# A plain step in the up projection, reserved buffers for the down projection, and x2 added earlier

## The chip, the cores and the metric

The kernel runs on one core of a Trainium2 chip. Its engines are TensorE (PE, with its weight loads shown apart as PEld), VectorE (DVE), ScalarE (ACT), GpSimd (POOL) and SyncE (SP, which here issues the DMAs). The metric is the device time of one execution in microseconds. Three runs of the kernel before took 2077.02, 2077.21 and 2078.11 us; the median is 2077.21.

## The reference

One decoder layer on 512 tokens of width 2048, all in float32. Two attentions (sliding window with sinks, and stick-breaking) share one input projection and one output projection, and behind them stands an MLP with squared ReLU:

```python
x = x + jnp.einsum('bse,ed->bsd', mix, w_out[l])
h = rmsnorm(x, norm_mlp_g[l])
u = jnp.einsum('bsd,df->bsf', h, w_up[l])
x = x + jnp.einsum('bsf,fd->bsd', jnp.square(jax.nn.relu(u)), w_down[l])
```

`w_up` is 2048 x 8192, `w_down` 8192 x 2048. The change lies in these two products. Below, x2 is the x that enters the MLP.

## The kernel before

Every float32 factor is split in two float32r parts, hi (a cast on ACT) and lo (the difference, on DVE; `split`, lines 88 to 90), and a product is made of three matmuls: hi x hi, hi x lo, lo x hi.

**Up projection** (lines 784 to 880). Both factors are cut in 2 x 2 blocks, and seven block products replace eight (the Strassen-Winograd scheme). There are G = 32 groups of 256 columns of `w_up`, and in each KP = 8 steps k, one for a pair of 128-row blocks. A step (`u_step`, line 833) does this: every second step issues the weight DMA for four pairs ahead (`u_load`, `st`) and POOL's four sums of weight blocks for two pairs ahead (`u_sums`, `s_`, two buffers); each step splits the weights of step i + 2 (`u_split`: three raw blocks, 128x384, and four sums, 128x512, four buffers of hi and lo in `whl`), then makes 21 matmuls of 256 columns (`u_products`). The other factor lies ready: `h2[k]` with seven blocks in hi and lo, made from x2 by `turn_x2` (line 731) by way of the buffer `hq`. It is scaled by a first estimate `rp` of the norm; the exact factor q2 is applied at the very end.

The four PSUM banks of group g - 1 are finished during the steps of group g: `u_finish` (line 798) is a generator that yields after each piece. It adds the banks up (`e`, `u`), applies ReLU and square on ACT, forms the sums for the next scheme (`a`), splits them (`ah` on ACT, `al` on DVE, 128x1792), and stores them in DRAM (`ac`).

**Down projection** (lines 885 to 1035). Again seven products, P1 to P7, over 2 x 2 blocks. There are NC = 8 chunks c of the 8192 rows, and two halves j of the columns; cj counts both. Each product is 24 matmuls of 512 columns (lines 1015 to 1025). `d_load` brings raw weight blocks (two DMAs of 1 MB for each r), `d_act` one block of activations (1 MB), `d_sum` makes T1 to T4 on POOL, `d_split` the hi and lo parts, one product ahead. `d_take` (line 930) adds a finished bank to the sums in SBUF, one product later. In the last chunk it also adds U2 to three of the four results, and `onto` (line 944) makes result x q2 + x2 on DVE. In that chunk the products P2, P3 and P4 are scaled by q2 as they are added, and the rows are stored.

**What sets the order.** The program is written for a scheduler that keeps dependencies, inserts the waits, and may reorder instructions on an engine; each engine then works strictly in its order. SBUF is handed out by pools, on two stacks, left and right. A pool that takes the place of closed pools waits for their last use. The pools of the down projection (`rw` for raw weights, `t3`, `ab` for activations) lie on the right, where `h2_0` to `h2_5` and the sums of the up projection were:

```python
    finishing = u_finish(G - 1, ps, ew)
    mlp.close()
    ...
    rw = ctx.enter_context(tc.tile_pool(name="rw", bufs=6, side="right", reuse_waits="tile"))
```

The first loads, T1 and the first split are written behind the whole up projection (lines 982 to 989), and the last group's `u_finish` behind the first product of the down projection (line 1027).

Of the kernel before, what the change touches and what calls it, by code (L numbers as in the profile page):

```python
# [20 lines left out]
P = 128  # L21
# [37 lines left out]
def hymba_layer(ctx: ExitStack, tc: tile.TileContext, x, norm_attn_g, w_in, q_norm_g, k_norm_g,  # L59
# [17 lines left out]
           0: even.enter_context(tc.tile_pool(name="big0", bufs=KD // 2))}  # L77
    once = attn.enter_context(tc.tile_pool(name="once", bufs=1, side="right"))
# [282 lines left out]
    oscr = dram.tile([2 * 8, P, T], F32, name="oscr")  # L361
    S = [once.tile([P, T], F32, name=f"S{b}") for b in range(2)]
# [347 lines left out]
    def evac_b(n, t, ps):  # L710
# [4 lines left out]
        junk = xw.tile([P, 512], F32, tag="junk", bufs=2, name=f"j2{n}{t}")  # L715
        nc.scalar.activation(out=junk, in_=xt, func=AF.Square, accum_out=ss2[:, t, n:n + 1])
        xts[n, t] = xt
# [8 lines left out]
        for tt in range(NT) if n == 0 else (t,):  # L726
            xs = xw.tile([P, 512], F32, tag="xs", bufs=8, name=f"xs2_{n}{tt}")
            nc.scalar.mul(out=xs, in_=xts[n, tt], mul=rp[:, tt:tt + 1])
            xts[n, tt] = xs

    def turn_x2(n, kk, banks):

        k = 2 * n + kk
        hq = xw.tile([P, 8, HP], F32, tag="hq", bufs=2, name=f"hq{k}")
        for r in range(2):
# [5 lines left out]
            nc.scalar.mul(out=hq[:, 0::7] if r == 0 else hq[:, 1:3],  # L741
                          in_=tr.rearrange("p (b t) -> p b t", b=2), mul=g)
        for o, a, b in ((3, 7, 0), (4, 2, 3), (5, 2, 7), (6, 1, 4)):
            nc.vector.tensor_tensor(out=hq[:, o], in0=hq[:, a], in1=hq[:, b], op=ALU.subtract)
        hi = hp[k].tile([P, 7, HP], F32R, name=f"h2h{k}")
        lo = hp[k].tile([P, 7, HP], F32R, name=f"h2l{k}")
        split(hq[:, 0:7], hi, lo)
# [36 lines left out]
    def u_products(i, ps):
# [3 lines left out]
        for a, b, n, half in U_PRODUCTS:  # L788
# [9 lines left out]
    def u_finish(g, ps, ew):  # L798
# [13 lines left out]
        nc.vector.tensor_tensor(out=e[:, 3], in0=u[:, 1], in1=y[:, 0], op=ALU.add)  # L812
        a = ew.tile([P, 8, HP], F32, tag="a", name=f"a{g}")
# [40 lines left out]
    odd.close()  # L854
    left = ExitStack()
# [12 lines left out]
    ms2 = sm.tile([P, NT], F32, tag="ms", name="ms_2")  # L868
    nc.vector.tensor_reduce(out=q2, in_=ss2, axis=AX.X, op=ALU.add)
    nc.vector.tensor_scalar(out=ms2, in0=q2, scalar1=1.0 / D, scalar2=EPS, op0=ALU.mult, op1=ALU.add)  # L870
    for _ in range(2):
        nc.vector.tensor_tensor(out=ms2, in0=ms2, in1=rp, op=ALU.mult)
    nc.vector.reciprocal(out=q2, in_=ms2)
    tail.close()
    ew = left.enter_context(tc.tile_pool(name="ew", bufs=1))
    for g in range(1, G):
        finishing = u_finish(g - 1, ps, ew)
        ps = u_banks(g)
        for i in range(g * KP, (g + 1) * KP):
            u_step(i, ps, finishing)  # L880
    finishing = u_finish(G - 1, ps, ew)
    mlp.close()
# [47 lines left out]
    def d_take(q, banks):  # L930
# [32 lines left out]
        if not last:  # L963
            return
# [15 lines left out]
    for cj in range(2 * NC):  # L980
        c, j = divmod(cj, 2)
        if cj == 0:
# [5 lines left out]
            for i in ORDER[1:]:  # L988
                d_act(0, i)
# [69 lines left out]
```

## Time and profile before

| What | Value |
|---|---|
| median of three runs | 2077.21 us |
| the profiled execution | 2076.19 us, of which the span is 2074.5 us |
| PE busy | 2019.0 us (97% of the span), 11652 matmuls |
| DVE busy | 1678.5 us (81%) |
| ACT, POOL busy | 1008.1 us (49%), 1045.7 us (50%) |
| up projection, groups 1 to 31 | about 774 to 1422.6 us |
| down projection | 1427.5 us to the end |

PE is busy nearly throughout, and matmuls overlap (each shows 283 ns where the next starts far earlier), so the busy share of PE says little: what counts is the distance of one matmul's start to the next. An idle time in brackets, or behind a bar, is that of the engine just ahead of the instruction, with what ended it. In the views by stretch the engines come in the order PE, PEld, DVE, ACT, POOL, and behind them the granted clock (1.00 is 2.4 GHz, 0.50 is 1.2), the DMA share and GB/s. The timeline gives starts in microseconds from the span's start. `lo_u` and `hi_u` are the split weights of the up projection, `s_u` POOL's sums, `st_u` raw weights; `lo_d`, `hi_d`, `T` and `st_d` are the same in the down projection, `ad` its activations, `C` and `U` its results, `x2r` a block of x2.

### The profile page before, as it was taken

How to read it: one execution, taken by the hardware profiler on the slowest of the kernel's cores; microseconds unless marked ns; L12 is line 12 of the kernel's file. 1: busy time of each engine (PE TensorE's matmuls, PEld its weight loads, DVE VectorE, ACT ScalarE, POOL GpSimd, SP SyncE). 2: the span in 40 equal slices, each digit the busy share in tenths (PEclk: the TensorE clock that was granted, in tenths of full speed). 3: DMA queues.
4: the chain of work that ended last, by engine and by line, in shares of the span. 5: the costliest groups of instructions: out<-in, count | busy, mean ns of one | idle time of the engine just before them, and what ended most of it. 6: DMA issues, size and time to landing. Idle time of an engine off the chain costs nothing. (4 is left out here: it accounts for less than half of the span.)

```text
span 2074.5 us, 30963 instructions
## 1 busy us (share of the span) xinstructions
PE 2019.0 (97%) x11652; PEld 1722.1 (83%) x11652; DVE 1678.5 (81%) x2038; ACT 1008.1 (49%) x1692; POOL 1045.7 (50%) x904
## 2 busy tenths in 40 slices
PE   8999999999999999999999999998999999999998
PEld 7777777777677889999999999997788888888876
DVE  4468646565775579999999999998889888988999
ACT  6267534544553565555555555554543333333332
POOL 0013322222220137777778787877755555555663
PEclk9999999999999999999999999999999999999999
DMA  6742332223345535656555555658756456456453
GB/s 217 116 133 82 102 96 73 72 92 117 103 140 175 180 109 163 195 186 194 187 188 194 185 196 184 198 183 326 265 208 230 158 206 244 144 204 260 152 187 108
DMA packets 213913, 350.28 MB, mean 169 GB/s; under 512 B 9779, under 2 KB 154372, under 8 KB 206596
## 3 DMA queue, kind: packets, MB, share of 16 engines
q1 hardware_dynamic: 211216, 345.02, 49.1%
q10 hardware_dynamic: 2548, 3.30, 1.4%
q8 instruction: 91, 1.49, 0.3%
q14 instruction: 58, 0.48, 0.1%
HBM read 270.16 MB, written 78.12 MB: 168 GB/s over the span
## 5 line engine op out<-in xcount | busy, mean ns | idle before, releaser
L794 PE MATMUL ps_u<-h2h,lo_u 128*128 128x256 f32 x1792 | 506.7, 283 | 15.7 <-DVE lo_u L90 15.7
L793 PE MATMUL ps_u<-h2l,hi_u 128*128 128x256 f32 x1792 | 506.4, 283 | 2.7 <-DVE h2l L90 2.7
L792 PE MATMUL ps_u<-h2h,hi_u 128*128 128x256 f32 x1792 | 506.3, 283 | 0.6 <-ACT h2h L89 0.6
L769 POOL TENSOR_TENSOR s_u<-st_u 128x256 f32<-128x256 f32 x256 | 254.6, 1015 | 242.3 <-DVE lo_u L90 171.7
L1024 PE MATMUL ps_d<-lo_d,ad 128*128 128x512 f32 x896 | 357.1, 399 | 6.4 <-DVE lo_d L90 6.4
L1023 PE MATMUL ps_d<-hi_d,ad 128*128 128x512 f32 x896 | 356.5, 398 | 6.5 <-DMA ad<-ac 4.9
L794 PEld LDWEIGHTS ps_u<-h2h,lo_u 128*128 128x128 f32 x1792 | 340.1, 190 | 21.9 <-DVE lo_u L90 21.8
L1025 PE MATMUL ps_d<-hi_d,ad 128*128 128x512 f32 x896 | 356.5, 398 | 0.0
L793 PEld LDWEIGHTS ps_u<-h2l,hi_u 128*128 128x128 f32 x1792 | 337.0, 188 | 3.2 <-DVE h2l L90 3.1
L792 PEld LDWEIGHTS ps_u<-h2h,hi_u 128*128 128x128 f32 x1792 | 336.6, 188 | 1.0 <-ACT h2h L89 1.0
L90 DVE TENSOR_TENSOR lo_d<-T,hi_d 128x1024 fp32r<-128x1024 f32 x128 | 244.8, 1924 | 49.4 <-ACT hi_d L89 49.4
L89 ACT CAST hi_u<-s_u 128x512 fp32r<-128x512 f32 x256 | 158.3, 618 | 226.4 <-POOL s_u L769 226.4
L918 POOL TENSOR_TENSOR T<-st_d,T 128x1024 f32<-128x1024 f32 x64 | 162.6, 2543 | 208.9 <-DVE lo_d L90 207.7
L90 DVE TENSOR_TENSOR lo_u<-s_u,hi_u 128x512 fp32r<-128x512 f32 x256 | 248.0, 969 | 8.6 <-ACT hi_u L89 8.4
L89 ACT CAST hi_d<-T 128x1024 fp32r<-128x1024 f32 x128 | 134.3, 1051 | 214.0 <-PE ps_d L1025 196.8
L1024 PEld LDWEIGHTS ps_d<-lo_d,ad 128*128 128x128 f32 x896 | 169.4, 189 | 49.9 <-DVE lo_d L90 8.9
L1023 PEld LDWEIGHTS ps_d<-hi_d,ad 128*128 128x128 f32 x896 | 169.6, 189 | 48.8 <-ACT a L816 4.9
L90 DVE TENSOR_TENSOR lo_u<-st_u,hi_u 128x384 fp32r<-128x384 f32 x256 | 202.3, 790 | 4.6 <-ACT hi_u L89 4.6
L1025 PEld LDWEIGHTS ps_d<-hi_d,ad 128*128 128x128 f32 x896 | 169.6, 189 | 41.1
L90 DVE TENSOR_TENSOR lo_d<-st_d,hi_d 128x1024 fp32r<-128x1024 f32 x96 | 190.1, 1996 | 13.3 <-ACT hi_d L89 13.2
L89 ACT CAST hi_d<-st_d 128x1024 fp32r<-128x1024 f32 x96 | 100.9, 1051 | 163.5 <-PE ps_d L1025 163.5
L769 POOL TENSOR_TENSOR s_u<-s_u,st_u 128x256 f32<-128x256 f32 x128 | 140.5, 1098 | 0.0
(220 smaller groups left out, 3823.6 us busy)
## 6 DMA issues: line engine op xcount, KB each, us to landing
st_u<-in_w_up SPq DMA_DIRECT2D x128, 512.0 KB, 4.4
st_d<-in_w_down SPq DMA_DIRECT2D x64, 1024.0 KB, 6.1
ad<-ac SPq DMA_DIRECT2D x56, 1024.0 KB, 6.4
ac<-ah SPq DMA_DIRECT2D x32, 896.0 KB
ac<-al SPq DMA_DIRECT2D x32, 896.0 KB, 4.8
st_qk<-in_w_in SPq DMA_DIRECT2D x64, 256.0 KB, 3.0
st_o<-in_w_out SPq DMA_DIRECT2D x32, 512.0 KB, 4.2
st_qa<-in_w_in SPq DMA_DIRECT2D x16, 512.0 KB, 3.8
```

Source lines behind the costliest of these rows:

```text
L89: nc.scalar.copy(out=hi, in_=st)
L90: nc.vector.tensor_tensor(out=lo, in0=st, in1=hi.bitcast(F32), op=ALU.subtract)
L769: nc.gpsimd.tensor_tensor(out=o, in0=a, in1=b, op=op)
L792: nc.tensor.matmul(o, wh[:, a], hh[:, b], start=first, stop=False, skip_group_check=True)
L793: nc.tensor.matmul(o, wh[:, a], hl[:, b], start=False, stop=False, skip_group_check=True)
L794: nc.tensor.matmul(o, wl[:, a], hh[:, b], start=False, stop=(k == KP - 1), skip_group_check=True)
L918: nc.gpsimd.tensor_tensor(out=o, in0=raw[cj, a, h], in1=raw[cj, b, h], op=ALU.subtract)
L1023: nc.tensor.matmul(o, al, bh[:, kk], start=first, stop=False, skip_group_check=True)
L1024: nc.tensor.matmul(o, al, bl[:, kk], start=False, stop=False, skip_group_check=True)
L1025: nc.tensor.matmul(o, ar, bh[:, kk], start=False, stop=end, skip_group_check=True)
```

## The change

- The step k = PLAIN = 7 of each up group uses eight plain block products in place of seven. `h2[7]` has four blocks, its weights are split as they are (one split of 128x512), POOL makes sums for k = 6 alone in that pair, and `u_finish` gets one more addition.
- Two weight buffers (`rwa`) and one activation buffer (`aba`) are set aside on the left from the start of the up projection; the right keeps four and six (`rwb`, `abb`). `hq` has one buffer instead of two, and the squares are written where `xs` goes later.
- The first weight loads, the first activation block, T1 and the first split are written into the steps 1, 4 and 6 of the last up group.
- x2, multiplied by t2 = 1/q2, is added to the sums after P2 of chunk 2, P3 of chunk 3, P4 of chunk 4 and P7 of chunk 5 (DVE); in the last chunk ACT scales the results by q2 in place.
- In the very last product the matmuls of the first bank come ahead of those of the second.
- Small tiles named pad shift what lies behind them.

```diff
+    edge = ctx.enter_context(tc.tile_pool(name="edge", bufs=1, side="right"))
+    edge.tile([P, 120], F32, name="pad_right")
...
+    const.tile([P, 32], F32, name="pad_left")
+    sm.tile([P, 32], F32, tag="pad", bufs=1, name="pad_small")
...
+    PLAIN = KP - 1
...
-        junk = xw.tile([P, 512], F32, tag="junk", bufs=2, name=f"j2{n}{t}")
-        nc.scalar.activation(out=junk, in_=xt, func=AF.Square, accum_out=ss2[:, t, n:n + 1])
+        xs = xw.tile([P, 512], F32, tag="xs", bufs=8, name=f"xs2_{n}{t}")
+        nc.scalar.activation(out=xs, in_=xt, func=AF.Square, accum_out=ss2[:, t, n:n + 1])
...
-        hq = xw.tile([P, 8, HP], F32, tag="hq", bufs=2, name=f"hq{k}")
+        hq = xw.tile([P, 8, HP], F32, tag="hq", bufs=1, name=f"hq{k}")
...
+        nb = 4 if k == PLAIN else 7
+        hi = hp[k].tile([P, nb, HP], F32R, name=f"h2h{k}")
+        lo = hp[k].tile([P, nb, HP], F32R, name=f"h2l{k}")
+        if k != PLAIN:
+            for o, a, b in ((3, 7, 0), (4, 2, 3), (5, 2, 7), (6, 1, 4)):
+                nc.vector.tensor_tensor(out=hq[:, o], in0=hq[:, a], in1=hq[:, b], op=ALU.subtract)
+        split(hq[:, 0:nb], hi, lo)
...
             s_ = sp.tile([P, 2, 4, P], F32, tag="s", name=f"s_u{i}")
+            if i % (KP // 2) == PLAIN // 2:
+                w, s_ = w[:, 0:1], s_[:, 0:1]
...
+            if i % KP == PLAIN:
+                split(w, hi[:, 0:4], lo[:, 0:4])
+                return
...
+    U_PLAIN = ((1, 0, 1, 0), (3, 1, 1, 0), (1, 3, 3, 0), (3, 2, 3, 0), (0, 0, 3, 1), (2, 1, 3, 1), (0, 3, 0, 1),
+               (2, 2, 0, 1))
...
-        for a, b, n, half in U_PRODUCTS:
+        for a, b, n, half in U_PLAIN if k == PLAIN else U_PRODUCTS:
...
         nc.vector.tensor_tensor(out=e[:, 3], in0=u[:, 1], in1=y[:, 0], op=ALU.add)
+        nc.vector.tensor_tensor(out=e[:, 3], in0=e[:, 3], in1=w[:, 1], op=ALU.add)
...
     odd.close()
+    rwa = ctx.enter_context(tc.tile_pool(name="rwa", bufs=2))
+    aba = ctx.enter_context(tc.tile_pool(name="aba", bufs=1))
     left = ExitStack()
...
-                st = rw.tile([P, 2, 1024], F32, tag="rw", name=f"st_d{cj}{r}{h}")
+                pool = rwa if (4 * cj + 2 * r + h) % 6 < 2 else rwb
+                st = pool.tile([P, 2, 1024], F32, tag="rw", name=f"st_d{cj}{r}{h}")
...
-            a = ab.tile([P, 2, 4, HP], F32R, tag="a", name=f"ad{c}{i}")
+            a = (aba if i == ORDER[0] else abb).tile([P, 2, 4, HP], F32R, tag="a", name=f"ad{c}{i}")
...
-            nc.vector.scalar_tensor_tensor(out=o, in0=o, scalar=q2[:, t:t + 1], in1=xt, op0=ALU.mult, op1=ALU.add)
+            nc.vector.scalar_tensor_tensor(out=o, in0=xt, scalar=t2[:, t:t + 1], in1=o, op0=ALU.mult, op1=ALU.add)
...
+            if (c, name) in ((2, "P2"), (3, "P3"), (4, "P4"), (5, "P7")):
+                onto(o, n, t)
         if not last:
             return
         for tt in range(2):
             if name == "P1":
-                n, t = column(0, tt, 0)
-                onto(sums_d["C11", j, tt], n, t)
+                o = sums_d["C11", j, tt]
+                nc.scalar.mul(out=o, in_=o, mul=q2[:, tt:tt + 1])
...
                     nc.gpsimd.tensor_tensor(out=o, in0=o, in1=sums_d["U2", j, tt], op=ALU.add)
-                    onto(o, n, t)
+                    nc.scalar.mul(out=o, in_=o, mul=q2[:, t:t + 1])
...
+    for g in range(1, G):
+        finishing = u_finish(g - 1, ps, ew)
+        ps = u_banks(g)
+        for k in range(KP):
+            if g == G - 1:
+                if k == 1:
+                    d_load(0, 0)
+                    d_act(0, ORDER[0])
+                elif k == 4:
+                    d_sum(0, "T1")
+                elif k == 6:
+                    d_split(0)
+            u_step(g * KP + k, ps, finishing)
+    finishing = u_finish(G - 1, ps, ew)
+    mlp.close()
+    rwb = ctx.enter_context(tc.tile_pool(name="rwb", bufs=4, side="right", reuse_waits="tile"))
+    t3 = ctx.enter_context(tc.tile_pool(name="t3", bufs=2, side="right", reuse_waits="tile"))
+    abb = ctx.enter_context(tc.tile_pool(name="abb", bufs=6, side="right", reuse_waits="tile"))
...
         if cj == 0:
-            d_load(0, 0)
-            d_act(0, ORDER[0])
-            d_sum(0, "T1")
-            d_split(0)
+            d_act(0, ORDER[1])
             d_load(0, 1)
-            for i in ORDER[1:]:
+            for i in ORDER[2:]:
                 d_act(0, i)
...
+            at_end = q == 14 * NC - 1
+            for h, tt in sorted(((h, tt) for h in range(2) for tt in range(2)), key=lambda x: x[::-1] if at_end else x):
+                bh, bl = parts_d[q, h]
```

## Rows read from the trace of the kernel before

**Rows 1.** The page's part 1: engine, busy us (share of the span), instructions.

```profile
PE 2019.0 (97%) x11652; PEld 1722.1 (83%) x11652; DVE 1678.5 (81%) x2038; ACT 1008.1 (49%) x1692; POOL 1045.7 (50%) x904
```

**Rows 2.** Busy time by stretch: window, length, engines' busy us, clock, DMA.

```profile
814.00:1422.60 608.60, 592.86 (x4892) 586.85 (x4891) 584.39 (x730) 337.58 (x579) 465.84 (x461) 1.00 0.59 190
1422.60:1485.00 62.40, 52.99 (x211) 41.50 (x210) 54.10 (x32) 30.24 (x35) 47.48 (x16) 0.95 0.91 357
1485.00:2018.00 533.00, 533.00 (x2276) 428.50 (x2276) 474.62 (x373) 203.24 (x198) 305.59 (x113) 1.00 0.54 200
2018.00:2074.50 56.50, 49.15 (x205) 37.83 (x204) 51.59 (x48) 14.70 (x14) 23.28 (x12) 0.99 0.36 112
```

**Rows 3.** The same view: parts of one up group, and the down projection's start.

```profile
1002.60:1022.55 19.95, 19.95 (x168) 19.95 (x167) 19.16 (x24) 11.12 (x19) 16.08 (x16) 1.00 0.57 185
1002.40:1023.25 20.85, 20.36 (x168) 20.16 (x168) 20.06 (x26) 11.65 (x20) 16.08 (x16) 1.00 0.58 189
1427.80:1431.20 3.40, 3.40 (x10) 2.63 (x9) 3.40 (x5) 2.33 (x3) 1.19 (x1) 0.50 1.02 411
```

**Rows 4.** Timeline of PE, up projection: start, us, operation, [idle before].

```profile
1002.41 0.38 PE L794 MATMUL ps_u<-h2h,lo_u 128*128 128x256 f32 x1 [0.48 <-DVE lo_u L90]
```

**Rows 5.** Waits of PE, 748 to 1423: us in total, times, longest.

```profile
PE ps_u L794 <- DVE lo_u L90: 15.7, 30, 1.4
PE ps_u L793 <- DVE h2l L90: 2.7, 2, 1.7
```

**Rows 6.** Timeline of DVE over the same group.

```profile
999.33 2.56 DVE L827 TENSOR_TENSOR al<-a,ah 128x1792 fp32r<-128x1792 f32 x1
1001.81 0.55 DVE L90 TENSOR_TENSOR lo_u<-st_u,hi_u 128x384 fp32r<-128x384 f32 x1
1002.28 0.68 DVE L90 TENSOR_TENSOR lo_u<-s_u,hi_u 128x512 fp32r<-128x512 f32 x1
1004.49 1.08 DVE L90 TENSOR_TENSOR lo_u<-st_u,hi_u 128x384 fp32r<-128x384 f32 x1
1011.67 0.41 DVE L812 TENSOR_TENSOR e<-u,ps_u 128x256 f32<-128x256 f32 x1
1014.49 0.43 DVE L818 TENSOR_TENSOR a<-a 128x256 f32<-128x256 f32 x1 [0.48 <-ACT a L816]
```

**Rows 7.** Groups by form, 814 to 1420: count, busy, mean ns, idle before.

```profile
L90 DVE TENSOR_TENSOR lo_u<-s_u,hi_u 128x512 fp32r<-128x512 f32 x232 | 225.8, 973 | 7.9 <-ACT hi_u L89 7.9
L90 DVE TENSOR_TENSOR lo_u<-st_u,hi_u 128x384 fp32r<-128x384 f32 x233 | 185.0, 794 | 0.0
L769 POOL TENSOR_TENSOR s_u<-st_u 128x256 f32<-128x256 f32 x230 | 224.9, 998 | 128.1 <-DVE lo_u L90 128.1
```

**Rows 8.** Waits of PE, 1422.6 to 1485.

```profile
PE ps_d L1023 <- DMA ad<-ac: 4.9, 2, 4.7
PE ps_d L1024 <- DVE lo_d L90: 2.9, 1, 2.9
PE ps_d L1023 <- ACT U L956: 1.6, 1, 1.6
```

**Rows 9.** Timeline of POOL and DVE around the start of the down projection.

```profile
1415.97 3.83 POOL L918 TENSOR_TENSOR T<-st_d 128x1024 f32<-128x1024 f32 x1 [4.38 <-DMA st_d<-in_w_down]
...
1417.49 2.72 DVE L90 TENSOR_TENSOR lo_u<-st_u,hi_u 128x384 fp32r<-128x384 f32 x1
...
1438.36 2.35 DVE L827 TENSOR_TENSOR al<-a,ah 128x1792 fp32r<-128x1792 f32 x1 [1.80 <-ACT ah L825]
```

**Rows 10.** Groups of DVE, forms apart, 1485 to 2010.

```profile
L948 DVE SCALAR_TENSOR_TENSOR C<-C,q,x2r 128x512 f32<-128x512 f32 x2 | 2.7, 1360 | 0.0
```

**Rows 11.** The end: waits of PE from 2010; timelines of DVE and PE.

```profile
PE ps_d L1024 <- DVE lo_d L90: 3.5, 4, 1.5
...
2015.94 5.19 DVE L948 SCALAR_TENSOR_TENSOR C<-C,q,x2r 128x512 f32<-128x512 f32 x3
...
2070.25 0.39 PE L1025 MATMUL ps_d<-hi_d,ad 128*128 128x512 f32 x1
```

More of the change, by code (lines that the diff above doesn't have):

```diff
@@ L726, in evac_b @@
         for tt in range(NT) if n == 0 else (t,):
-            xs = xw.tile([P, 512], F32, tag="xs", bufs=8, name=f"xs2_{n}{tt}")
-            nc.scalar.mul(out=xs, in_=xts[n, tt], mul=rp[:, tt:tt + 1])
+            xt, xs = xts[n, tt]
+            nc.scalar.mul(out=xs, in_=xt, mul=rp[:, tt:tt + 1])
             xts[n, tt] = xs
@@ L740, in turn_x2 @@
             g = gT[:, 16 + 2 * k + r:17 + 2 * k + r]
-            nc.scalar.mul(out=hq[:, 0::7] if r == 0 else hq[:, 1:3],
+            nc.scalar.mul(out=hq[:, 1:3] if r else hq[:, 0:4:3] if k == PLAIN else hq[:, 0::7],
                           in_=tr.rearrange("p (b t) -> p b t", b=2), mul=g)
[L743 to L747, printed above, removed]
+        nb = 4 if k == PLAIN else 7
[5 more added lines that the diff above has]
+        split(hq[:, 0:nb], hi, lo)
         h2[k] = hi, lo
@@ L867, in hymba_layer @@
     q2 = const.tile([P, NT], F32, name="q2")
-    ms2 = sm.tile([P, NT], F32, tag="ms", name="ms_2")
+    t2 = const.tile([P, NT], F32, name="t2")
     nc.vector.tensor_reduce(out=q2, in_=ss2, axis=AX.X, op=ALU.add)
-    nc.vector.tensor_scalar(out=ms2, in0=q2, scalar1=1.0 / D, scalar2=EPS, op0=ALU.mult, op1=ALU.add)
+    nc.vector.tensor_scalar(out=t2, in0=q2, scalar1=1.0 / D, scalar2=EPS, op0=ALU.mult, op1=ALU.add)
     for _ in range(2):
-        nc.vector.tensor_tensor(out=ms2, in0=ms2, in1=rp, op=ALU.mult)
-    nc.vector.reciprocal(out=q2, in_=ms2)
+        nc.vector.tensor_tensor(out=t2, in0=t2, in1=rp, op=ALU.mult)
+    nc.vector.reciprocal(out=q2, in_=t2)
     tail.close()
     ew = left.enter_context(tc.tile_pool(name="ew", bufs=1))
[L876 to L882, printed above, removed]
     NC = G // 4
-    rw = ctx.enter_context(tc.tile_pool(name="rw", bufs=6, side="right", reuse_waits="tile"))
-    t3 = ctx.enter_context(tc.tile_pool(name="t3", bufs=2, side="right", reuse_waits="tile"))
-    ab = ctx.enter_context(tc.tile_pool(name="ab", bufs=7, side="right", reuse_waits="tile"))
     wd = w_down.rearrange("(g r p) n -> r p g n", r=2, p=P)
@@ L894, in hymba_layer @@
                   ("P4", 2, "T4", 3, True))
+    ORDER = [p[1] for p in D_PRODUCTS]
     def d_load(cj, r):
@@ L973, in d_take @@
                     nc.gpsimd.tensor_tensor(out=o, in0=o, in1=sums_d["U2", j, tt], op=ALU.add)
-                    onto(o, n, t)
+                    nc.scalar.mul(out=o, in_=o, mul=q2[:, t:t + 1])
                     if target == "C22":
                         done(o, n, t)
-    ORDER = [p[1] for p in D_PRODUCTS]
+    for g in range(1, G):
[16 more added lines that the diff above has]
+    abb = ctx.enter_context(tc.tile_pool(name="abb", bufs=6, side="right", reuse_waits="tile"))
     before = None
@@ L1014, in hymba_layer @@
             a = act[c, ai]
-            for h in range(2):
-                bh, bl = parts_d.pop((q, h))
-                for tt in range(2):
-                    ts = slice(tt * P, (tt + 1) * P)
-                    for kk in range(2):
-                        al, ar = a[:, 0, 2 * h + kk, ts], a[:, 1, 2 * h + kk, ts]
-                        o = banks[b][tt]
-                        first, end = h == 0 and kk == 0 and not more, h == 1 and kk == 1
-                        nc.tensor.matmul(o, al, bh[:, kk], start=first, stop=False, skip_group_check=True)
-                        nc.tensor.matmul(o, al, bl[:, kk], start=False, stop=False, skip_group_check=True)
-                        nc.tensor.matmul(o, ar, bh[:, kk], start=False, stop=end, skip_group_check=True)
+            at_end = q == 14 * NC - 1
+            for h, tt in sorted(((h, tt) for h in range(2) for tt in range(2)), key=lambda x: x[::-1] if at_end else x):
+                bh, bl = parts_d[q, h]
+                ts = slice(tt * P, (tt + 1) * P)
+                o = banks[b][tt]
+                for kk in range(2):
+                    al, ar = a[:, 0, 2 * h + kk, ts], a[:, 1, 2 * h + kk, ts]
+                    first, end = h == 0 and kk == 0 and not more, h == 1 and kk == 1
+                    nc.tensor.matmul(o, al, bh[:, kk], start=first, stop=False, skip_group_check=True)
+                    nc.tensor.matmul(o, al, bl[:, kk], start=False, stop=False, skip_group_check=True)
+                    nc.tensor.matmul(o, ar, bh[:, kk], start=False, stop=end, skip_group_check=True)
             before = q, banks
```

7 lines of the change are left out of this document (4 added, 3 removed).

## The prediction

> **What bounds the kernel now.** The page comes first: TensorE (PE) is busy 97% of the span, so only time in which PE starts no matmul can be won, and each added matmul costs its pitch [rows 1]. The stretches show where PE loses time [rows 2]. The up projection is the long one: 608.60 us with VectorE (DVE) at 96%, so two engines sit near their limit there. From 1422.60 to 1485.00, where the down projection begins, PE makes only 211 matmuls. From 1485 to 2018 it is never idle: 2276 matmuls in 533 us, a pitch of 0.234 us for 512 columns. In the last 56.5 us it again falls back.
>
> Inside one group of the up projection the pitch is 19.95 us over 167 weight loads, one for each matmul, so 0.1195 us, and 168 matmuls take 20.07 us [rows 3]. The group's period is 20.85 us, the window from one late matmul to just ahead of the next [rows 3, 4]. So 0.78 us of each group is a stall, at the third matmul of the step k = 7, which waits for `lo_u` from DVE. The waits count 30 of these [rows 5], one a group, the longest (1.4 us of idle) in group 31, so 29 are of the common kind.
>
> DVE's order explains the place [rows 6]: the 2.56 us `al` stands directly ahead of the split of k = 7, and PE resumes as the 0.55 us `lo_u` ends (1002.36). DVE is not idle before it; it arrives late since its whole round is 20.06 us of work [rows 3] and two waits for ACT, 0.48 us [rows 6] and 7.9 us in 29 groups, 0.27 us each [rows 7].
>
> **The plain step (k = 7): PE.** Eight products instead of seven, three matmuls each: 3 x 32 groups = 96 matmuls x 0.1195 = +11.5 us. This is certain; no cover exists.
>
> **The plain step: DVE and POOL.** One 128x512 subtraction replaces 0.55 + 0.68 us, so -0.55 us per group where it counts, directly behind `al` [rows 6]. The new sum into e[3] has L812's form and length, 0.41 us [rows 6]; it cannot be covered, DVE being in order. POOL's sums for the pair k = 6, 7 halve in width: four operations near 1 us [rows 7] become about 0.5, some 2 us less of POOL's 16.08 us per group [rows 3]. A DVE split costs 0.55 us with POOL idle and 1.08 us beside it [rows 6]; over the 16 splits of a group the means 973 and 794 ns [rows 7] against 0.68 and 0.55 are 8 x 0.29 + 8 x 0.24 = 4.3 us for 16.08 us of POOL, so 2 us less POOL gives DVE 0.5 us. And the k = 7 split needs no sum any more, so POOL's buffer comes free before `al` and not after it (POOL idles 128.1 us in the up projection waiting for such releases, and its sums are then what ACT and so DVE wait the 0.27 us for [rows 7]). DVE's round: 20.06 + 0.75 of waits = 20.8; -0.55 + 0.41 - 0.5 - 0.27 = 19.9 us. PE's round: 171 x 0.1195 = 20.43 us. PE becomes the bound with 0.5 us to spare, and the stall goes: 29 x 0.78 = -22.6 us. Bounds: nothing regained (0), all of it (-22.6); I take -22.6, because the relief sits at the very place of the stall. If DVE did not gain from POOL its round would be 20.7 us, which is a rival below.
>
> A rule of the Trainium skill speaks to this: "SBUF — State Buffer", section "SBUF: two separate sides", says that VectorE and GpSimd share a port pair under an exclusive lock, so that an operation with two SBUF inputs stands still until the other engine's whole instruction is over. The trace agrees in kind: 0.55 against 1.08 us [rows 6]. By it the halved sums help more than in proportion, and the moved T1 sums, which are long, hurt more (the second rival).
>
> **Group 0.** h2 of k = 7 has four blocks instead of seven and no subtractions. PE waited 2.7 us for `h2l` twice [rows 5], about half of it for k = 7. One `hq` buffer instead of two makes that preparation begin only after the split of k = 6. I take -1 us, between -1.5 and +1.5. Dropping the scratch tile of the squares moves no work.
>
> **Up to down.** The 211 matmuls from 1422.60 to 1485.00 need 211 x 0.234 = 49.4 us, so 13 us are lost [rows 2]: 4.7 us waiting for the activations `ad` (4.9 with a second, short wait), 2.9 for `lo_d`, 1.6 for ACT's copy of U2 [rows 8], and two stretches at a granted clock of 0.50, the level of 1.2 GHz, behind the first two of these waits. The one shown lasts 3.4 us [rows 3]; with columns at half the rate (0.43 us a matmul for 0.234) it loses 1.5 us. The reserved buffers let SP issue the two weight loads and the first activation block in step k = 1 of group 31; T1 and the first split follow at k = 4 and 6. On SP's queue only the stores of group 30's activations and the further loads come behind these three. The first product then starts without its wait: -4.8 and the slow clock behind it -1.5, with small second waits -0.4. What is late next: T3. Its weights (r = 1) still need the freed right side, and DVE and ACT must first finish group 31: relu, squares, `al` ended only 18 us after the up projection's last matmul [rows 9]. That chain starts no earlier, while PE now comes 5 us sooner, so I leave a T3 wait of 2 to 3 us, its slow clock and the copy of U2 as they are. Sum -7.5 us with some relief of T3; between -1 (all turned into later waits) and -13.
>
> **x2 in the middle chunks.** Sixteen `onto` operations leave chunk 7 for chunks 2 to 5, a pair at each of eight places. A DVE pair there costs 2.7 us, and the only pair that lay between 1485 and 2010 cost PE no idle time [rows 2, 10]. So 0; upper bound eight times the longest wait that such operations made at the end, 1.5 us [rows 11]: +12. The x2 loads are SP's and have a product's time ahead.
>
> **The last chunk and the end.** PE should need 205 x 0.234 = 48.0 us from 2018 to its last matmul at 2070.25 [rows 11]; it takes 52.3, so 4.3 us are lost, in 4 waits for `lo_d`, when DVE is held by `onto` (5.19 us for three [rows 11]). These go; the scaling on ACT, idle three quarters of that time [rows 2], replaces them. I take -4; between -4.5 and 0 (ACT's casts stand in order behind scalings that wait for POOL). The changed order of the last product leaves one store after the last matmul as now: 0.
>
> **Sum.** +11.5 - 22.6 - 1 - 7.5 - 4 = -23.6 us. The profiled execution took 2076.2 us (the span of 2074.5 and 1.7 around it), 1 us under the median of the runs; 2077.2 - 23.6 = 2053.5 us.
>
> **Rivals.**
> - DVE still bounds the up projection: POOL's relief doesn't reach it, its round is 20.7 us, 0.3 us above PE's. For: DVE was at 96%. Against: the k = 7 split leaves the POOL chain. 29 x 0.27 = +8: 2061 us. Chance 0.17.
> - The early loads only move the wait: T1's two POOL sums lie in group 31 beside its splits, where one such sum of 3.83 us already held a 0.55 us split for 2.72 us and PE for 1.4 [rows 9, 5]; two may hold DVE for 4 us (twice 2.72 - 0.55), and T3 stays late. Gain 1 instead of 7.5: 2060 us. The lock that the Trainium skill states in "SBUF — State Buffer", section "SBUF: two separate sides", would make this the likelier course. Chance 0.15.
> - The x2 pairs each stall PE by the 1.5 us of the end: +12, 2066 us. For: DVE is busy 474.62 of 533 us there [rows 2]. Against: the pair that cost nothing. Chance 0.08.
> - Slower than before: the stall is local, set by `al` standing ahead of the k = 7 split, not by DVE's load. Then it grows by the sum (0.41) and the wider first operation (0.13): 29 x 0.54 = +15.7 in place of -22.6; 2053.5 + 38.3 = 2092 us. It decides from 0.8 us of stall left per group, where the gains elsewhere are eaten. Against: DVE's late arrival is its full round, and the split ahead of PE's need would have 1 to 2 us in hand once it starts with the group. Chance 0.1.
>
> **How the numbers follow.** Forecast 0.5, its own range 2046 to 2058. Until 2 in 10 are left out the range must take in the first two rivals and most of the third: 2044 to 2070. Within 0.2% (4 us, about what a measurement here tells from none) needs several rivals together: 0.04. Slower: the last rival, 0.1. Faster: 0.86.
>
> **What would show it.** Right: group period 20.4 us, no PE wait for `lo_u` in groups 1 to 30, DVE under 95%; the first `ps_d` matmul within 0.5 us of the last `ps_u`; no wait for `lo_d` after 2018's counterpart; no gap in chunks 2 to 5. Wrong: periods above 20.7 us, PE waits at k = 7, or a granted clock of 0.5 at the start of the down projection.

## The result, and the profile after

The changed kernel takes 2044.05 us (median of 4 runs, 2043.11 to 2045.78); the kernel before, in the same comparison, 2077.66 us (2077.02 to 2078.21). The ratio is 0.9839, with a 95% interval from 0.9822 to 0.9856: 33.6 us faster, where 23.6 were forecast. The time lies inside the range given (2044 to 2070), but at its lowest edge, and the likeliest case's own range (2046 to 2058) misses it by 2 us. So the first question is where 10 more came from. The span fell from 2074.5 to 2041.0 us. The rows that answer to [rows 1]:

```profile
PE 2004.0 (98%) x11748; PEld 1725.3 (85%) x11748; DVE 1626.8 (80%) x2034; ACT 1014.5 (50%) x1676; POOL 1020.3 (50%) x904
```

PE starts 96 matmuls more and is nevertheless busy for 15 us less. The busy time by stretch of the kernel after, with the columns of [rows 2, 3] (the up groups, one group, the last group, a part of it, and the middle of the down projection):

```profile
814.00:1376.00 562.00, 562.00 (x4723) 561.24 (x4722) 508.51 (x685) 318.32 (x524) 420.28 (x440) 1.00 0.60 194
1002.60:1022.90 20.30, 20.30 (x174) 20.30 (x173) 18.38 (x26) 11.54 (x19) 15.27 (x16) 1.00 0.61 196
1376.70:1406.50 29.80, 23.52 (x173) 23.02 (x172) 27.61 (x27) 11.88 (x17) 22.38 (x14) 0.89 0.47 169
1397.80:1404.60 6.80, 5.87 (x27) 5.87 (x28) 5.57 (x6) 4.45 (x4) 2.85 (x2) 0.50 0.27 92
1506.00:1958.00 452.00, 452.00 (x1946) 364.65 (x1945) 419.99 (x343) 172.89 (x167) 261.76 (x92) 1.00 0.57 210
```

In the up groups PE no longer has an idle time that a view shows, and DVE's share went from 96% to 90.5% (508.51 of 562.00). The last group, though, takes 29.8 us for 23.5 of work, and a part of it runs at a granted clock of 0.50.

The timeline gives each matmul's start (168 a group before, 171 after; 24 a product), and from these the two traces split as follows (a product is 24 matmuls of the down projection, a period the time from one group's first matmul to the next). The forecast's terms are spread over the same stretches; the 11.5 us of added matmuls are 0.36 a group.

| Stretch | before, us | after, us | change | forecast |
|---|---|---|---|---|
| up to the first matmul of the up projection | 748.19 | 740.86 | -7.3 | 0 |
| groups 0 and 1 | 47.74 | 45.64 | -2.1 | -0.3 |
| groups 2 to 30 (period 20.859, then 20.353) | 604.91 | 590.24 | -14.7 | -12.2 |
| group 31, up to the first matmul of the down projection | 26.63 | 29.82 | +3.2 | -7.1 with the next |
| first 16 products | 98.59 | 92.69 | -5.9 | |
| next 80 products | 449.83 | 446.24 | -3.6 | 0 |
| last 16 products and the rest | 98.59 | 95.56 | -3.0 | -4 |

Two rows stand against the forecast: 7.3 and 3.6 us came in stretches to which no term was given, and the way from up to down brought 2.7 us, not 7.1. The groups of DVE and POOL by form, 800 to 1370, answer to [rows 6, 7]:

```profile
L92 DVE TENSOR_TENSOR lo_u<-st_u,hi_u 128x384 fp32r<-128x384 f32 x196 | 155.2, 792 | 0.0
L92 DVE TENSOR_TENSOR lo_u<-s_u,hi_u 128x512 fp32r<-128x512 f32 x195 | 155.2, 796 | 0.0
L845 DVE TENSOR_TENSOR al<-a,ah 128x1792 fp32r<-128x1792 f32 x28 | 56.7, 2025 | 18.4 <-ACT ah L843 18.4
L92 DVE TENSOR_TENSOR lo_u<-st_u,hi_u 128x512 fp32r<-128x512 f32 x28 | 34.3, 1225 | 0.0
L836 DVE TENSOR_TENSOR a<-a 128x256 f32<-128x256 f32 x28 | 18.2, 650 | 32.2 <-ACT a L834 32.2
L830 DVE TENSOR_TENSOR e<-e,ps_u 128x256 f32<-128x256 f32 x28 | 11.8, 421 | 1.0
```

The split of four sums fell from 973 to 796 ns and `al` from 2560 to 2025. DVE now waits 50.6 us for ACT (18.4 and 32.2), 1.8 us a group where it was 0.75.

The list of PE's waits from 770 to 1376 is empty, yet the period is 20.31 us up to group 20 and 20.46 from group 22 on. Two pairs of rows show why: DVE's first split of a group, and the first matmul of PE that reads it, in groups 10 and 28.

```profile
946.40 1.09 DVE L92 TENSOR_TENSOR lo_u<-st_u,hi_u 128x384 fp32r<-128x384 f32 x1
949.19 0.28 PE L811 MATMUL ps_u<-h2h,lo_u 128*128 128x256 f32 x1
...
1314.50 1.10 DVE L92 TENSOR_TENSOR lo_u<-st_u,hi_u 128x384 fp32r<-128x384 f32 x1
1315.65 0.39 PE L811 MATMUL ps_u<-h2h,lo_u 128*128 128x256 f32 x1
```

In group 10 the split is ready 1.7 us ahead of PE, in group 28 PE starts 0.05 us behind its end. DVE's round, its waits for ACT included, is 20.45 us ((1314.50 - 946.40) / 18), longer than PE's 20.31; its lead, the time that a split is ready before PE reads it, falls by 0.15 us a group, and once it is spent DVE bounds the groups again. These waits are so short that they hide under the row of the matmul ahead, and the list does not show them. What the list has for PE from 1376 to 1500, then from 1958 on (total, times, longest):

```profile
PE ps_u L811 <- DVE lo_u L92: 6.3, 2, 5.4
PE ps_d L1053 <- ACT U L969: 1.6, 1, 1.6
PE ps_d L1053 <- DMA ad<-ac: 1.4, 1, 1.4
...
PE ps_d L1054 <- DVE lo_d L92: 1.2, 2, 0.8
PE ps_d L1053 <- ACT hi_d L91: 0.3, 1, 0.3
```

The waits for `ad` (4.9) and `lo_d` (2.9) of [rows 8] are down to 1.4 and none. In their place stands one for `lo_u`, of 5.4 us, in group 31, that the kernel before had at 1.4 [rows 5]. Three timelines show how it comes about. POOL, three of its T sums (the second of T1, the first of T2, the second of T3):

```profile
1385.25 2.38 POOL L931 TENSOR_TENSOR T<-st_d 128x1024 f32<-128x1024 f32 x1
...
1393.26 2.53 POOL L931 TENSOR_TENSOR T<-st_d,T 128x1024 f32<-128x1024 f32 x1
1395.75 2.52 POOL L931 TENSOR_TENSOR T<-st_d,st_d 128x1024 f32<-128x1024 f32 x1
```

DVE over the same time, where the second of these rows is a sum of activations in `u_finish`:

```profile
1385.91 2.14 DVE L92 TENSOR_TENSOR lo_u<-st_u,hi_u 128x384 fp32r<-128x384 f32 x1
...
1393.51 2.56 DVE L839 TENSOR_TENSOR a<-a 128x256 f32<-128x256 f32 x1
1395.99 2.69 DVE L92 TENSOR_TENSOR lo_u<-st_u,hi_u 128x384 fp32r<-128x384 f32 x1
```

PE, from the first of its two waits to the down projection's first matmul:

```profile
1388.10 0.38 PE L811 MATMUL ps_u<-h2h,lo_u 128*128 128x256 f32 x1 [0.89 <-DVE lo_u L92]
...
1398.73 0.58 PE L811 MATMUL ps_u<-h2h,lo_u 128*128 128x256 f32 x1 [5.40 <-DVE lo_u L92]
1399.11 0.41 PE L809 MATMUL ps_u<-h2h,hi_u 128*128 128x256 f32 x1
...
1406.43 0.28 PE L811 MATMUL ps_u<-h2h,lo_u 128*128 128x256 f32 x1
1406.55 0.40 PE L1053 MATMUL ps_d<-hi_d,ad 128*128 128x512 f32 x1
```

Each of these DVE operations starts beside a T sum and ends 0.3 to 0.4 us behind it: a subtraction of 256 elements takes 2.56 us, a split of 384 takes 2.69 us where it takes 0.55 alone. PE resumes as the second split ends; behind the 5.4 us it runs at the lower clock, 1.2 GHz, for 6.8 us (0.21 us from start to start instead of 0.12). Then the down projection follows the up projection with no gap.

### The profile page after: what moved, and what is told of

Same layout as the page of the kernel before. It is cut to its first block, busy times and chain, and to the rows that moved or that the text cites. A ratio compares the mean times of both kernels' runs of the same rounds, so it can differ in the third digit from the quotient of the medians.

```text
span 2041.0 us, 31132 instructions
## 1 busy us (share of the span) xinstructions
PE 2004.0 (98%) x11748; PEld 1725.3 (85%) x11748; DVE 1626.8 (80%) x2034; ACT 1014.5 (50%) x1676; POOL 1020.3 (50%) x904
## 5 line engine op out<-in xcount | busy, mean ns | idle before, releaser
L811 PE MATMUL ps_u<-h2h,lo_u 128*128 128x256 f32 x1824 | 515.9, 283 | 6.3 <-DVE lo_u L92 6.3
L810 PE MATMUL ps_u<-h2l,hi_u 128*128 128x256 f32 x1824 | 514.7, 282 | 2.4 <-DVE h2l L92 2.4
L809 PE MATMUL ps_u<-h2h,hi_u 128*128 128x256 f32 x1824 | 514.8, 282 | 0.1
L810 PEld LDWEIGHTS ps_u<-h2l,hi_u 128*128 128x128 f32 x1824 | 346.6, 190 | 2.9 <-DVE h2l L92 2.8
L809 PEld LDWEIGHTS ps_u<-h2h,hi_u 128*128 128x128 f32 x1824 | 346.6, 190 | 0.3 <-ACT h2h L91 0.3
L779 POOL TENSOR_TENSOR s_u<-st_u 128x256 f32<-128x256 f32 (+1 forms) x256 | 200.1, 801 | 252.3 <-DVE lo_u L92 181.2
L92 DVE TENSOR_TENSOR lo_u<-st_u,hi_u 128x384 fp32r<-128x384 f32 (+1 forms) x256 | 218.2, 853 | 4.4 <-ACT hi_u L91 4.3
L92 DVE TENSOR_TENSOR lo_u<-s_u,hi_u 128x512 fp32r<-128x512 f32 x224 | 178.1, 795 | 1.0 <-ACT hi_u L91 1.0
L91 ACT CAST hi_u<-s_u 128x512 fp32r<-128x512 f32 x224 | 138.5, 618 | 78.7 <-POOL s_u L779 78.6
L779 POOL TENSOR_TENSOR s_u<-st_u,s_u 128x256 f32<-128x256 f32 (+1 forms) x128 | 167.8, 1311 | 10.0
```

The costliest lines, as they stand in the source:

```text
L91: nc.scalar.copy(out=hi, in_=st)
L92: nc.vector.tensor_tensor(out=lo, in0=st, in1=hi.bitcast(F32), op=ALU.subtract)
L779: nc.gpsimd.tensor_tensor(out=o, in0=a, in1=b, op=op)
L809: nc.tensor.matmul(o, wh[:, a], hh[:, b], start=first, stop=False, skip_group_check=True)
L810: nc.tensor.matmul(o, wh[:, a], hl[:, b], start=False, stop=False, skip_group_check=True)
L811: nc.tensor.matmul(o, wl[:, a], hh[:, b], start=False, stop=(k == KP - 1), skip_group_check=True)
```

## The experiments

Theory behind the prediction: the up groups are bound by DVE, whose round the plain step and POOL's relief shorten. Rivals: the time comes from the pads, that is from where the operands lie; POOL's relief does not matter; the early loads turn their win into a wait inside group 31. Each run was compared with the kernel before, on the same chip. That kernel took 2076.84 to 2078.24 us in the five comparisons, so the difference of two experiments can be off by about 1 us. "Period" is the mean of groups 2 to 30.

**1. The pads alone**, in the kernel before (so large that every tile lies modulo 512 bytes as in the changed kernel):

```diff
+    edge.tile([P, 120], F32, name="pad_right")
...
+    const.tile([P, 40], F32, name="pad_left")
+    sm.tile([P, 32], F32, tag="pad", bufs=1, name="pad_small")
```


> The kernel before with nothing but the small pad tiles, sized so that every pool starts at the same address modulo 512 bytes as in the changed kernel. Theory (placement): the start address of the tiles that PE reads sets the distance between matmuls. Then the part ahead of the up projection takes 7.3 us less (the distance falls from 0.232 to 0.227 us), the down projection some 5 us less, and the up groups nothing, since DVE holds them at 20.85 us: about 2065 us. Rival: the pads do nothing and the 7 us ahead of the up projection come from an order of instructions that the other edits brought: 2077 us.

2068.21 us, ratio 0.9952 (0.9936 to 0.9969). The first up matmul starts at 740.50 us instead of 748.19, a middle product takes 5.60 instead of 5.62 us, the group period stays (20.90 us; the waits for `lo_u` from 770 to 1376 are 28 of together 19.3 us, 0.69 each, where one was 0.48 before). So placement is worth 9 us here, and the up projection cannot use it while DVE is its bound.

**2. The change without the pads** (t2 takes a place that was there before):

```diff
-    edge.tile([P, 120], F32, name="pad_right")
...
-    const.tile([P, 32], F32, name="pad_left")
-    sm.tile([P, 32], F32, tag="pad", bufs=1, name="pad_small")
```


> The changed kernel without its pad tiles, and with t2 in a place that moves nothing, so that pools start at the addresses modulo 512 of the kernel before. Theory (placement): 7.3 us come back ahead of the up projection, 4 in it (5472 matmuls at 0.1196 instead of 0.1188 us), 5 in the down projection: about 2060 us. Rival (pads do nothing): 2044 us.

2055.13 us, 0.989 (0.9876 to 0.9905). All that the prediction priced is worth 22.5 us (2077.67 - 2055.13); the pads add 11. Period 20.457 us and no gap; group 31 takes 26.40 us, the first 16 products 93.76.

**3. The plain step alone**, in the kernel before:

```diff
+        for a, b, n, half in U_PLAIN if k == PLAIN else U_PRODUCTS:
...
+            if i % (KP // 2) == PLAIN // 2:
+                w, s_ = w[:, 0:1], s_[:, 0:1]
```


> The kernel before with the plain step k = 7 and nothing else. Forecast's step: DVE's round falls under PE's, the stall at k = 7 goes, groups take 171 x 0.1195 = 20.43 us: -0.41 x 30 = -12 us, 2065 us. Rival (POOL's relief doesn't reach DVE): 20.7 us a group, 2072 us. Rival (the stall is local to al): groups of 21.7 us, 2104 us.

2067.79 us, 0.9952 (0.9938 to 0.9967). Period 20.460 us, against the 20.43 that the prediction gave PE, and the waits of PE from 770 to 1376 are an empty list. The stall is gone by the step itself. The whole run gains 10 us, not the 12.1 of these terms (11.5 - 22.6 - 1), since the start of the down projection loses: its first 16 products take 103.49 us for 98.59.

**4. The changed kernel with POOL's sums at full width** in every pair, the halves for the plain step read by nothing:

```diff
-            if i % (KP // 2) == PLAIN // 2:
-                w, s_ = w[:, 0:1], s_[:, 0:1]
```


> The changed kernel with POOL's sums at full width for the pair of the plain step too; the second half is not used. Forecast's step: POOL's relief gives DVE 0.5 us of each round, so without it DVE's round is 20.4 us against 20.31 of PE's, and little is lost: 0 to 0.15 us a group, 2044 to 2049 us. Rival (the relief is what lifted the bound): groups of 20.7 us and more, 2056 us.

2063.18 us, 0.9933 (0.9916 to 0.9949): 19 us of the gain are lost, more than the rival gave. Groups 1 to 5 still take 20.31 us, and from group 7 on the period is 21.1 us. Its DVE groups by form, 800 to 1370:

```profile
L92 DVE TENSOR_TENSOR lo_u<-s_u,hi_u 128x512 fp32r<-128x512 f32 x189 | 172.5, 913 | 0.0
L92 DVE TENSOR_TENSOR lo_u<-st_u,hi_u 128x384 fp32r<-128x384 f32 x189 | 163.3, 864 | 0.0
L843 DVE TENSOR_TENSOR al<-a,ah 128x1792 fp32r<-128x1792 f32 x27 | 54.7, 2025 | 17.8 <-ACT ah L841 17.8
```

The waits of PE, 770 to 1376:

```profile
PE ps_u L809 <- DVE lo_u L92: 12.5, 24, 0.6
```

The two splits take 117 and 72 ns more than in the changed kernel, 7 x 0.189 = 1.3 us a group, and PE waits again, once a group. `al` stays at 2025 ns, so the narrower sums are not what shortened it.

**5. The first loads, T1 and the first split written behind the loop again:**

```diff
-            if g == G - 1:
-                if k == 1:
-                    d_load(0, 0)
...
+            d_load(0, 0)
+            d_act(0, ORDER[0])
+            d_sum(0, "T1")
+            d_split(0)
```


> The changed kernel with the first loads, T1 and the first split written where they were before, behind the up projection; the reserved buffers stay. Forecast's step: what the early loads gain comes back, 7.5 us: 2051.5 us. Rival (the wait has only moved into group 31, which takes 29.8 us in the changed kernel and 26.6 with the first gap in the one before): no more than 2 us come back, 2046 us, and group 31 loses its 5.4 us stall.

2043.17 us, 0.9832 (0.9817 to 0.9847), the same as the changed kernel, group 31 included (29.61 us). The forecast's step is refuted. The rival's time holds, but not its sign: group 31 keeps its 5.4 us wait. The scheduler places the loads and sums in the same order from either place in the program, so the reserved buffers are the whole edit.

**6. x2 and the last scaling as before:**

```diff
-            if (c, name) in ((2, "P2"), (3, "P3"), (4, "P4"), (5, "P7")):
-                onto(o, n, t)
...
-                    nc.scalar.mul(out=o, in_=o, mul=q2[:, t:t + 1])
+                    onto(o, n, t)
```


> The changed kernel with x2 and the scaling as before: onto on DVE in the last chunk, nothing in chunks 2 to 5. Forecast's step: the end loses its 4 us again and the middle gains nothing: 2048 us, the last 16 products back from 91.4 to 94 us. Rival (the middle pairs had stalled PE): the products of chunks 2 to 5, 5.60 us each now, get shorter and the time stays near 2044 us.

2047.61 us, 0.9857 (0.9843 to 0.9872). The 80 middle products take 446.24 us with the additions and without; the last 16 take 95.35 instead of 91.38. So the edit is worth 4.0 us at the end and costs nothing in the middle, as forecast.

**7. Activations at the edge of the right side**, weights and T behind them, so that the second weights come later and T3 cannot run in group 31:

```diff
+    abb = ctx.enter_context(tc.tile_pool(name="abb", bufs=6, side="right", reuse_waits="tile"))
     rwb = ctx.enter_context(tc.tile_pool(name="rwb", bufs=4, side="right", reuse_waits="tile"))
     t3 = ctx.enter_context(tc.tile_pool(name="t3", bufs=2, side="right", reuse_waits="tile"))
-    abb = ctx.enter_context(tc.tile_pool(name="abb", bufs=6, side="right", reuse_waits="tile"))
```


> The changed kernel with the right-hand pools of the down projection in another order: the activations at the edge, where the first up blocks come free, and the weights further in, so that the weights with r = 1 land later and POOL's T3 and T2 can't run inside group 31. Theory (POOL's long sums hold DVE's splits in group 31): the 5.4 us stall and the slow clock behind it go, group 31 falls from 29.8 to 21 or 22 us, the wait of 1.4 us for activations goes too, and part comes back as a later wait for T3 (up to 5 us): 2036 to 2041 us. Rival (the stall comes from T1 alone, or from DVE's own work): group 31 stays above 27 us, 2043 us.

2046.47 us, 0.9851 (0.9836 to 0.9865), outside the theory's 2036 to 2041. Group 31 falls, as it said, to 21.73 us, and the third product takes 15.72 instead of 5.60. The timeline of POOL has T3's first sum at:

```profile
1405.84 2.39 POOL L931 TENSOR_TENSOR T<-st_d,st_d 128x1024 f32<-128x1024 f32 x1 [17.06 <-DMA st_d<-in_w_down]
```

The waits of PE from 1370 to 1480:

```profile
PE ps_d L1054 <- DVE lo_d L92: 7.4, 3, 6.2
PE ps_d L1053 <- DMA ad<-ac: 1.7, 1, 1.7
PE ps_d L1053 <- ACT U L969: 1.6, 1, 1.6
PE ps_u L811 <- DVE lo_u L92: 0.9, 1, 0.9
```

Without T3's and T2's sums group 31 has only the 0.9 us wait beside T1: these sums are what holds DVE there. The time only moves, for now the weights come late, and the third product takes 10 us longer where the theory allowed 5.

**8. The same with four activations at the edge and two behind T3**, to let T3 run between the two cases:

```diff
+    abx = ctx.enter_context(tc.tile_pool(name="abx", bufs=4, side="right", reuse_waits="tile"))
     rwb = ...
     t3 = ...
-    abb = ctx.enter_context(tc.tile_pool(name="abb", bufs=6, side="right", reuse_waits="tile"))
+    abb = ctx.enter_context(tc.tile_pool(name="abb", bufs=2, side="right", reuse_waits="tile"))
```


> The changed kernel with the second to fifth activation blocks at the right edge and the weights with r = 1 behind them: those weights wait for step k = 4 of group 31 and queue behind four activation blocks, not six. Theory (the long sums of T3 and T2 hold DVE in group 31, and in the run with all six activations first they only came too late): T3 runs around the end of group 31, group 31 takes 21 to 23 us instead of 29.8, and the third product waits less than the 10 us that it waited there: 2036 us (2032 to 2042). Rival (DMA is the limit, whatever the order): what group 31 gains, the third product loses again, 2043 to 2047 us.

2047.24 us, 0.9855 (0.9839 to 0.9872): a miss for the theory. Group 31 again takes 21.73 us, the third product 17.92; T3's first sum waits for its weights:

```profile
1407.48 2.39 POOL L931 TENSOR_TENSOR T<-st_d,st_d 128x1024 f32<-128x1024 f32 x1 [17.14 <-DMA st_d<-in_w_down]
```

**9. The activations of the down projection 480 bytes further on**, at byte 32 modulo 512 as the split weights:

```diff
+    shift.tile([P, 120], F32, name="pad_abb")
     abb = ctx.enter_context(tc.tile_pool(name="abb", bufs=6, side="right", reuse_waits="tile"))
```


> The changed kernel with 480 bytes more ahead of the activation blocks, so that they start at 32 modulo 512 like the split weights, as the one reserved block already does, whose products take 5.45 us where the others take 5.60. Theory (placement): the other 96 products fall to 5.45 too: -14 us, 2030 us. Rival (the 5.45 us come from the reserved block's place on the left, or from its being the first product): 2044 us.

2031.44 us, 0.9778 (0.9763 to 0.9793): as expected, and 13 us below the changed kernel. Every middle product takes 5.44 us, 435.20 instead of 446.24 for the 80. The stretch that stands last in the table of after, in this kernel:

```profile
1506.00:1958.00 452.00, 452.00 (x1996) 374.28 (x1995) 434.41 (x349) 177.61 (x171) 272.25 (x96) 1.00 0.58 216
```

1996 matmuls instead of 1946 in the same 452 us, at the same clock, PE never idle in either.

**10. The same with the left side at byte 0** (its pad 24 floats, not 32), so that activations and split weights differ again:

```diff
-    const.tile([P, 32], F32, name="pad_left")
+    const.tile([P, 24], F32, name="pad_left")
```


> The run with the activations at 32, but the whole left side (split weights among it) moved from 32 to 0 modulo 512. Theory (what counts is the start modulo 64 of weights and moving operand together, 32 with 32 being best for 512 columns): the part ahead of the up projection goes back to 0.232 us a matmul (+7 us), the down projection to 5.6 us a product (+16 us), the up steps to 2.49 us: 2055 us. Rival (a start at a multiple of 512 is best): no part gets slower, 2031 us or less.

2045.03 us, 0.9842 (0.9827 to 0.9856). Neither forecast holds. Middle products are back at 5.60 us, as the theory had it, but for those of the reserved buffer, which lies at 0 with the weights (5.45). Groups take 20.52 us, longer and not shorter, and the stretch ahead of the up projection keeps its gain (741.14). Group 31 takes 25.64 us.

**11. Experiments 8 and 9 together**, with `h2_6` and `h2_7` at byte 0 as the other `h2`:

```diff
+    gap.tile([P, 120], F32, name="pad_h2")
...
+    shift.tile([P, 120], F32, name="pad_abb")
+    abx = ctx.enter_context(tc.tile_pool(name="abx", bufs=4, side="right", reuse_waits="tile"))
```


> The run before this one, with the activation blocks at 32 modulo 512 (which brought 13 us) and h2 of k = 6 and 7 moved from 32 to 0 modulo 512, where the steps k = 0 to 5 have theirs and take 2.485 us instead of 2.517. By placement: 2036 - 13 - 2 = 2021 us. Rival: the later loads gain nothing, 2029 us; if h2's start is not what sets those steps, they stay at 2.52 us.

2033.01 us, 0.9785 (0.977 to 0.9799). Products 5.44 us; groups 20.23 us up to group 13, 20.46 from 15 on; the third product 18.08 us. This is a miss, 12 us above the forecast and 4 above the rival. T3's place again returns what it saves, and the earlier matmuls of groups 1 to 13 win nothing: groups 2 to 30 take 590.66 us, in experiment 9 590.30. DVE's lead is only spent sooner.

**12. T3 on the place of the up projection's last sums**, with both shifts of experiment 11:

```diff
     rwb = ...
-    t3 = ctx.enter_context(tc.tile_pool(name="t3", bufs=2, side="right", reuse_waits="tile"))
     abb = ...
+    t3 = ctx.enter_context(tc.tile_pool(name="t3", bufs=2, side="right", reuse_waits="tile"))
```


> The third product's sums (T3) get the place where the up projection's last sums lie, so that they cannot start before group 31's last split; the activations of the down projection start at byte 32 modulo 512, as the weights do, and h2_6 and h2_7 at 0 modulo 512. Theory (DVE's wait inside group 31 comes from the T sums that run on POOL there, and two of these are T3's): the stretch from group 31's first matmul to the down projection's first falls from 28.8 to between 24 and 27 us, the groups take 20.23 us as where h2_6 and h2_7 last stood at 0; 2026 to 2030 us in all. Rival (POOL then takes T2's first sum inside group 31 instead, which holds DVE's split just as long): that stretch stays near 29 us, 2030 to 2031 us.

2028.94 us (2027.98 to 2030.38), 0.977 (0.9753 to 0.9786), the fastest of all; its runs just touch those of experiment 9 (2030.13 to 2032.63). The time is in the theory's range, but group 31 takes 27.94 us, between the two forecasts. The waits of PE for the up projection's splits, 1376 to 1480, and the two longest of them:

```profile
PE ps_u L811 <- DVE lo_u L92: 5.5, 3, 3.5
...
1396.04 0.39 PE L811 MATMUL ps_u<-h2h,lo_u 128*128 128x256 f32 x1 [1.12 <-DVE lo_u L92]
1402.26 0.39 PE L811 MATMUL ps_u<-h2h,lo_u 128*128 128x256 f32 x1 [3.47 <-DVE lo_u L92]
```

POOL's timeline, T2's first sum and both of T3, and DVE's beside the latter:

```profile
1392.04 2.86 POOL L933 TENSOR_TENSOR T<-st_d,T 128x1024 f32<-128x1024 f32 x1
1396.66 4.99 POOL L933 TENSOR_TENSOR T<-st_d,st_d 128x1024 f32<-128x1024 f32 x2 [1.77 <-DVE lo_u L92]
...
1396.96 2.49 DVE L840 TENSOR_TENSOR a<-a 128x256 f32<-128x256 f32 x1
1399.37 2.84 DVE L92 TENSOR_TENSOR lo_u<-st_u,hi_u 128x512 fp32r<-128x512 f32 x1
```

T2's first sum moves into group 31, as the rival said, and costs the wait of 1.12 us. The longest wait, 3.47 us, is still behind T3's sums: they now start behind the last split of sums, but the plain step's split, which needs no sums, comes later and is held. PE waits 0.8 us less in all (5.5 for 6.3).

## Why the prediction was right or wrong

- **PE's price and the stall: right; the room behind it: wrong.** Without the pads the period is 20.457 us, 0.03 from the forecast. Groups 2 to 30 won 11.7 us there (29 x 0.402), of 12.2 forecast; that DVE's lateness is its whole round, not `al` alone, is borne out by experiments 3 and 4, and the slower rival with it refused. But "with 0.5 us to spare" fails: DVE's round is 20.45 us, not 19.9. Its work is 18.4 us, 1.0 less than the sum had, but its waits for ACT are 1.8 us a group where 0.48 were left to them, and shorter idle times make up the rest. Without the pads that is just PE's round, and the splits of k = 0 stay 3.1 to 3.4 us ahead of PE. With the pads PE is faster than DVE, and the first rival (DVE still bounds) holds for the last ten groups, at 0.15 us each.
- **POOL's relief: the right mechanism, mis-sized.** "2 us less POOL gives DVE 0.5 us" should have read 1.3 by experiment 4. Between the two traces it is 1.5: DVE's busy time in a group fell from 20.06 [rows 3] to 18.38 us, and the split for split (-0.54) and the new sum (+0.42) were priced rightly. The rest is 7 x 0.18 on the splits of sums, 0.53 on `al`, less 0.22 on L836: 1.55. `al` is as short with the plain step alone (2026 ns in experiment 3), and not by the narrower sums (experiment 4); that the split without sums is the reason is likely, not shown. Experiment 4 shows what hangs on the relief: without the narrower sums DVE bounds the groups again, as the first rival said. The forecast spread POOL's cost evenly over its busy time; what counts is which operations of the two start beside each other. The Trainium skill, "SBUF — State Buffer", section "SBUF: two separate sides", has a VectorE operation with two SBUF inputs and a GpSimd operation that reads SBUF exclude each other for a whole instruction, and this trace agrees (2.69 for 0.55 us beside a T sum).
- **From up to down: this step failed.** "The first product then starts without its wait: -4.8 and the slow clock behind it -1.5": it does start without (0.12 us behind the last up matmul), but 2.7 us were won of 7.1, and 5.1 without the pads (26.40 + 93.76 for 26.63 + 98.59). The second rival is what happened, with one correction: not T1's sums hold DVE most, but T3's and T2's, which the prediction had kept late. Their weights come early too: once the first two loads have places of their own, the next two find freed ones while group 31 still runs (issued 22 us ahead of the down projection's first matmul, 7 us in the kernel before). So the third product, to which the prediction left a wait for T3 of 2 to 3 us, falls from 10.34 to 5.60 us, and the price is paid in group 31. The two waits in group 31 cost 6.3 us and the slow clock behind them some 2.6 more (from 1398.73 to 1404.64 28 matmuls at 0.21 us instead of 0.12). Experiments 7 and 8 by their traces: without these sums group 31 has 0.9 us of wait left. The pads made it worse: without them DVE enters group 31 with a lead of 3.4 us, PE waits 3.5 us there and the group takes 26.40 us; with them the lead is spent, PE waits 6.3 us and it takes 29.82. Experiment 10, where PE needs 20.52 us a group and the lead stays at 3.4 us, has 3.5 us of wait and 25.64 again.
- **Reserved buffers, not written order.** The prediction followed the calls in steps 1, 4 and 6; experiment 5 shows that they change nothing.
- **Group 0**: -2.3 us against -0.6 (its -1 and 0.36 for the matmuls); the step's reason failed: the two waits for `h2l` are nearly as they were, together 2.4 us (2.7 [rows 5]), the longest 1.5 (1.7). What went is a stretch at the lower clock between them (granted clock 0.50 from 769.1 to 771.9), some 1.6 us: 15 matmuls at 0.20 us and more where they take 0.12. With it went most of a wait of 0.6 us for ACT. Group 0 before and after:

```profile
748.19:775.82 27.63, 24.29 (x185) 23.50 (x184) 23.77 (x32) 17.96 (x34) 13.49 (x12) 0.94 0.31 96
740.86:766.19 25.33, 22.82 (x189) 22.21 (x187) 20.84 (x30) 17.49 (x34) 10.81 (x14) 1.00 0.62 198
```

- **x2 in the middle, the end: right**, 0 and 4.0 by experiment 6 (3.0 between the two traces).
- **What was to show it.** Period 20.4, DVE under 95%, the first `ps_d` at once, no gap in the middle chunks: all there. "No PE wait for `lo_u` in groups 1 to 30" holds by the list of waits, but from group 22 on PE starts late by some 0.15 us a group. Of the waits for `lo_d` at the end 1.2 us are left; a granted clock of 0.50, named as a sign against, stands one stretch earlier than named, in group 31.
- **The pads: not priced at all.** They are worth 11.1 us (2055.13 - 2044.05): 22.5 of 23.6 came without them. The prediction's first sentence, "only time in which PE starts no matmul can be won", is the premise that failed: PE's distance from start to start fell too. Stretch by stretch, the pads win 7.9 us ahead of the up projection, 4.1 in the first 96 products, and nothing in the up projection, where 3.0 us in groups 2 to 30 come back as 3.4 in group 31.
- **Where it was luck.** That the time lies in the range hangs on 0.05 us. And the 22.5 us without the pads come near 23.6 since errors cancel: groups 0 and 1 gave 1.9 us more than forecast, from up to down 2.0 and the end 1.2 less.

That DVE's lead is spent also tells why the period rises from about group 21 on, and in experiments 11 and 12, where PE needs 20.23 us and the lead falls by 0.23 us a group, from group 14.

## What to carry to other kernels

When two engines share a limit, price a lighter one by the operations of the other that start beside it, not by its busy time; and when a load is made earlier, look at every operation that it sets free, and at what runs on the engine that this one excludes. Where PE is never idle, its distance from start to start is still open to placement: try where the operands start before removing work. And compare the rounds of two engines over many groups: an empty list of waits can mean that the slower one still lives on a lead.

## What the runs showed of the hardware

The distance between matmuls depends on where the two operands start in SBUF, at a granted clock of 1.00 and without an idle gap. The places are given in bytes modulo 512; that 512 is the period of the effect, no run tests. For 512 columns: 5.44 us for 24 matmuls with both at 32 (0.227 each), 5.45 with both at 0, 5.60 with one at 32 and one at 0, 5.62 at 384 and 480. For 256 columns it is another order: a group of 171 matmuls takes 20.23 us with the 128x128 operand at 32 and the other at 0 (0.1183 each), 20.52 with both at 0, 20.46 without the pads (384, and the other at 480 for six steps and 256 for two). These places were worked out from how the pools lie and stand in no trace; what in the chip makes the difference, no run here tells.

A VectorE subtraction with two SBUF inputs that starts beside a GpSimd sum of 128x1024 (2.5 us) ends just behind it: 2.69 us for 0.55 alone.
